# Channel mixer in 1024-column groups, two of eight k-pairs with seven block products

## The chip, the cores and the metric

One core of one Trainium2 chip runs the whole kernel. The metric is the device time of one execution in microseconds (us). Three runs of the kernel before gave 2060.73, 2060.61 and 2063.79 us; their median is 2060.73.

## The reference, cut to what matters

Two decoder layers work on 256 tokens of width 2048 (layer A: sliding-window attention, layer B: block attention over a shared K/V; both with memory heads), each followed by a dense squared-ReLU channel mixer with 8192 hidden columns. The change lies in the mixer and in the normalisation:

```python
h = layer_norm(ALPHA * h + mix, ln_g[layer, 0], ln_b[layer, 0])
ffn = jnp.square(jax.nn.relu(h @ w_up[layer])) @ w_down[layer]
h = layer_norm(ALPHA * h + ffn, ln_g[layer, 1], ln_b[layer, 1])
```

All data are f32.

## The kernel before, in words

**Precision by splitting.** Every operand of a product is kept as a sum of two fp32r tiles: `hi`, a cast made by ScalarE (ACT), and `lo = src - hi`, made by VectorE (DVE); `split` is lines 93 to 95. A product of two blocks takes three matmuls, x_hi w_hi, x_hi w_lo and x_lo w_hi (lines 169 to 171).

**Weights.** `weights` (line 97) fetches 1 MB with one DMA on SyncE's queue (SP) into a `raw` buffer of 128x2048, of which there are four (NRAW), and splits it as two halves of 1024 columns into `whi` and `wlo` buffers, of which there are seven each (NHI). A `raw` buffer is free when its splits are done, a `whi` or `wlo` buffer when its last matmul is done.

**Mixer.** The hidden width is cut into four chunks of 2048 columns (loop at line 482). In a chunk, four up passes (`aform`, line 158) multiply the transposed activations hT (16 k-tiles of 128) with 512 columns each, for both token tiles t = 0 and 1 in two PSUM banks of the pool `ps_mm` (four banks). One weight DMA covers four k-tiles of 512 columns: 24 matmuls. `relu2` (line 383) takes a bank through a ReLU on ACT and a square on DVE into a `u_n` buffer; four PE transposes per tile, placed by the hooks two and five k-tiles into the next pass, bring it into gT through a bank of the pool `ps_at` (four banks), with a cast on ACT and a subtraction on DVE (`transposed`, lines 323 to 330). Four down passes then multiply gT with the matching rows of w_down, and `residual` (line 332) adds each bank into h on DVE. A chunk has 768 matmuls of 512 columns and 32 transposes.

**Normalisation.** `ln_stat` (line 300) computes the inverse root of the variance with three Newton steps on 128x1 tiles: seven GpSimd (POOL) instructions, lines 310 to 314, between two DVE stages. There are four normalisations with two token tiles each. During two of them memory projections (a filler) keep TensorE (PE) at work; in layer 1's first one, and in the last, some of the matmuls of token tile 1 are held back (`hold`) for the same purpose.

**Order.** The tile framework plans each engine's queue at compile time, from the program's order as priority and from what is ready and which buffers are free in its own model; on the chip each queue of ACT, DVE and SP is worked off in that fixed order.

Of the kernel before, what the change touches and what calls it, by code (L numbers as in the profile page):

```python
# [8 lines left out]
F32 = mybir.dt.float32  # L9
# [23 lines left out]
FAR = -1e33  # L33
NRAW = 4
NHI = 7
NLG = 3
HOLD = 13
HOLDF = 14

# [25 lines left out]
WHOOKS = (10, 14, 4)  # L65
NWARM = 2
FILL = (10, 11, 12, 16)
UHOOKS = (2, 5)
WTAIL = ((1, 2), (2, 0), (3, 1), (5, 2), (7, 1), (9, 2))


# [1 line left out]
def trunk(ctx: ExitStack, tc: tile.TileContext, a: dict, out: bass.AP):  # L73
# [19 lines left out]
    def split(hi, lo, src):  # L93
        nc.scalar.copy(hi, src)  # L94
        nc.vector.tensor_tensor(lo, src, hi.bitcast(F32), ALU.subtract)  # L95

    def weights(src, parts=1):

# [59 lines left out]
    def aform(srcs, xts, hold=0, hooks={}):  # L158

        ps = [ps_mm.tile([P, 512], F32, name="ps_a", tag="mm") for _ in range(NT)]
        n = len(srcs)

        def mms(t, k, hi, lo):
            xh = xts[k // 4][:, k % 4, 0, t * P:(t + 1) * P]
            xl = xts[k // 4][:, k % 4, 1, t * P:(t + 1) * P]
            st, en = k == 0, k == 4 * n - 1
            nc.tensor.matmul(ps[t], xh, hi, start=st, stop=False)  # L169
            nc.tensor.matmul(ps[t], xh, lo, start=False, stop=False)  # L170
            nc.tensor.matmul(ps[t], xl, hi, start=False, stop=en)  # L171

        late = []
        for i, src in enumerate(srcs):
            halves = weights(src)
            for q in range(4):
                hi, lo = halves[q // 2]
                c = slice((q % 2) * 512, (q % 2) * 512 + 512)
                args = (4 * i + q, hi[:, c], lo[:, c])
                hooks.get(4 * i + q, nothing)()  # L180
                mms(0, *args)
                if 4 * i + q >= 4 * n - hold:
                    late.append(args)
                else:
                    mms(1, *args)

        def finish():
            for args in late:
                mms(1, *args)

        return ps, finish


    def evict_v(ps, nm):
# [105 lines left out]
    def ln_stat(stats):  # L300

        mv = sm.tile([P, 2], F32, name="mvar", tag="mvar")
        nc.vector.bn_aggr(mv, stats)
        v = sm.tile([P, 1], F32, name="v", tag="v")
        nc.vector.tensor_scalar(v, mv[:, 1:2], EPS, None, op0=ALU.add)
        y = sm.tile([P, 1], F32, name="y", tag="y")
        nc.vector.tensor_scalar(y.bitcast(I32), v.bitcast(I32), -0.5, 1597463007.0,
                                op0=ALU.mult, op1=ALU.add)
        w = sm.tile([P, 1], F32, name="w", tag="w")
        nc.gpsimd.tensor_scalar(w, v, -0.5, None, op0=ALU.mult)  # L310
        u = sm.tile([P, 1], F32, name="u", tag="u")
        for _ in range(3):
            nc.gpsimd.tensor_scalar(u, y, y, w, op0=ALU.mult, op1=ALU.mult)  # L313
            nc.gpsimd.tensor_scalar(y, u, 1.5, y, op0=ALU.add, op1=ALU.mult)
        return mv[:, 0:1], y

    def ln_apply(ht, mean, rstd, rows, j):
# [20 lines left out]
    def new_stats():  # L338
        return [sm.tile([P, 4, 6], F32, name=f"st{t}", tag=f"st{t}", bufs=2) for t in range(NT)]
# [4 lines left out]
    def normed(h, st, li, ps, finish, first, filler):  # L344


        if filler:
            rows = ln_rows(li, [[(wp, "raw", NRAW, D)]] * 2)
        else:
            rows = ln_rows(li, [[(ap_, "mk", 1, 1024), (ap_, "mv", 1, 1024)],  # L350
                                [(ap_, "v", 1, 1024)] + [(ap_, "pts", 2, 512)] * 2])
        xt = []
        if filler:
            finish()
            for t in range(NT):
                residual(h, ps, t, 3, first, st)
                mean, rstd = ln_stat(st[t])
                for j in range(4):
                    ln_apply(h[t], mean, rstd, rows, j)
            done = 0  # L360
            for j, at in enumerate(FILL):
                for _ in range(done, at):
                    next(filler)
                done = at
                xt.append(act_tile("hT", "hT", j))
                for t in range(NT):
                    transposed(h[t][:, j * 512:(j + 1) * 512], xt[j], t, j)
            for _ in filler:
                pass
            return xt  # L370
        for j in range(4):
            xt.append(act_tile("hT", "hT", j))
        for t in range(NT):
            if t:
                finish()
            residual(h, ps, t, 3, first, st)
            mean, rstd = ln_stat(st[t])
            for j in range(4):
                ln_apply(h[t], mean, rstd, rows, j)
                transposed(h[t][:, j * 512:(j + 1) * 512], xt[j], t, j)  # L380
        return xt

    def relu2(ps):

        u = ap_.tile([P, 512], F32, name="u_n", tag="lg", bufs=NLG)
        nc.scalar.activation(u, ps, AF.Relu)
        nc.vector.tensor_tensor(u, u, u, ALU.mult)
        return u
# [59 lines left out]
    for l in range(LAYERS):  # L448
        more = l + 1 < LAYERS
        wq, wk, wv, wqm = (a[f"{n}{l}"] for n in ("wq", "wk", "wv", "wqm"))  # L450
        ps, _ = aform([wv[0, i] for i in range(4)], hT, hooks={6: lambda: next(mem["mk_rest"])})
        v = evict_v(ps, "v")
        ot = new_acts("og", "ot")
        pipe = Stages()
        kt = None
        for g in range(KVH):
            kt = ap_.tile([P, T], F32, name="kt", tag="kt", bufs=2)
            wform_sum(wk[g], hT, kt, pipe.hooks(*WHOOKS))
            for hd in range(g * GROUP, (g + 1) * GROUP):
                qt = new_q()  # L460
                wform_sum(wq[hd], hT, qt, pipe.hooks(*WHOOKS))
                pipe.add(self_head(ot, hd, qt, kt, v, dist_a if l == 0 else dist_b, l == 0))
        if l == 0:
            for t in range(NT):
                h.append(ap_.tile([P, D], F32, name=f"h{t}", tag=f"h{t}"))
                nc.sync.dma_start(h[t], a["x"][t * P:(t + 1) * P, :])
        for m in range(MH):
            qt = new_q()
            wform_sum(wqm[m], hT, qt, pipe.hooks(*WHOOKS))
            pipe.add(mem_head(ot, m, qt, mem["mk"][:, m], mem["mv"]))  # L470
        if more:
            memt = load_acts(a["memt"], "hT", "memt")
        st = new_stats()
        for nb in range(4):
            ps, fin = aform([a["wo"][l, nb, i] for i in range(4)], ot, hold=(0 if nb < 3 else 8 if more else HOLD),
                            hooks=pipe.tail() if nb == 0 else {})
            if nb < 3:
                for t in range(NT):
                    residual(h, ps, t, nb, True, st)
        hT = normed(h, st, 2 * l, ps, fin, True, mem_v(l + 1, memt, mem) if more else None)  # L480
        st = new_stats()
        for c in range(FF // CH):
            gt = new_acts("og", "gT")
            todo = {}
            for nb in range(CH // 512):
                split_t = c == 0 and nb == 0 and not more
                ps, fin = aform([a["wup"][l, c * (CH // 512) + nb, i] for i in range(4)], hT,
                                hold=(16 if split_t else 0), hooks=todo)
                if split_t:
                    u0 = relu2(ps[0])  # L490
                    fin()
                    us = [u0, relu2(ps[1])]
                else:
                    us = [relu2(ps[t]) for t in range(NT)]
                todo = {UHOOKS[t]: (lambda u=us[t], g=gt[nb], t=t: transposed(u, g, t, 0)) for t in range(NT)}
            last = c == FF // CH - 1
            if last and more:
                memt = load_acts(a["memt"], "hT", "memt")
            for nb in range(4):
                end = last and nb == 3  # L500
                ps, fin = aform([a["wdn"][l, nb, 4 * c + i] for i in range(4)], gt,
                                hold=(0 if not end else 8 if more else HOLDF),
                                hooks=(todo if nb == 0 else {}))
                if not end:
                    for t in range(NT):
                        residual(h, ps, t, nb, c == 0, st if last else None)
        if more:
            hT = normed(h, st, 2 * l + 1, ps, fin, False, mem_k(l + 1, memt, mem))
    rows = ln_rows(2 * LAYERS - 1, [[(ap_, f"hT{i}", 1, D)] for i in range(2)])
# [52 lines left out]
```

## Time and profile before

| | us |
|---|---|
| median of three runs | 2060.73 |
| the profiled execution | 2060.95 |
| its span, first to last instruction | 2059.2 |
| granted clock of PE (mean) | 0.996 |

The span is 1.75 us shorter than the time of the same execution. Busy times overlap between engines; a PE record is longer than the distance to the next one, because matmuls are pipelined, so PE's pace is read from start times.

### The profile page before, as it was taken

To read this page: it belongs to the slowest core of one execution; us is meant where nothing else is said; L and a number is where in the kernel's file an instruction comes from. 1 tells how busy PE (TensorE), PEld (TensorE's weight loads), DVE (VectorE), ACT (ScalarE), POOL (GpSimd) and SP (SyncE) were. 2 spreads that over 40 slices of the span, in tenths; PEclk is the share of its full clock that TensorE was granted. 3 is DMA by queue.
4 is the path that set the end of the run, shared out by engine and by line. 5 is a ranking of instruction groups with operands and counts; after the bars stand their busy time and mean duration, and the time that the engine had idled before them with its cause. 6 is when DMAs were issued, how large, how long until landed. Compare 5 with 4: busy or idle time off the path is not lost.

```text
span 2059.2 us, 23603 instructions
## 1 busy us (share of the span) xinstructions
PE 2035.7 (99%) x9500; PEld 1695.2 (82%) x9500; DVE 1176.3 (57%) x1373; ACT 913.2 (44%) x1136; POOL 28.4 (1%) x64
## 2 busy tenths in 40 slices
PE   9999999999999999999999999899999999999997
PEld 7888888888888888888888888788888888888886
DVE  6566657555555555456575665665555555555555
ACT  6555435443443444345344554344344434434441
POOL 0000000000000000000010000100000000000001
PEclk9999999999999999999999999999999999999998
DMA  9644546555555555556554446355555555555651
GB/s 337 255 147 157 200 152 256 181 196 186 186 186 200 184 185 193 194 184 225 199 208 176 154 156 212 123 204 184 194 194 184 185 199 188 185 186 195 230 186 62
DMA packets 56269, 391.60 MB, mean 190 GB/s; under 512 B 6368, under 2 KB 6368, under 8 KB 9696
## 3 DMA queue, kind: packets, MB, share of 16 engines
q1 hardware_dynamic: 56160, 390.10, 53.4%
q8 instruction: 74, 1.21, 0.2%
q14 instruction: 35, 0.29, 0.0%
HBM read 387.98 MB, written 2.10 MB: 189 GB/s over the span
## 4 chain that ended last, share of the span: by engine, by line
PE 95%; DVE 3%; POOL 1%; issue 0%; DMA 0%; SPq 0%; ACT 0%; POOLq 0%; DVEq 0%
PE ps_a L169 26%; PE ps_a L171 26%; PE ps_a L170 26%; PE ps_w L147 7%; PE ps_w L149 4%; PE pt_h L327 2%; PE ps_m L405 1%; PE ps_m L404 1%; PE ps_m L406 1%; DVE h L321 1%; POOL u L313 1%; PE po L234 1%; PE pt L229 1%; PE ps_s L245 1%; DVE wlo L95 0%; DVE h L320 0%
## 5 line engine op out<-in xcount | busy, mean ns | idle before, releaser
L95 DVE TENSOR_TENSOR wlo<-raw,whi 128x1024 fp32r<-128x1024 f32 (+1 forms) x706 | 859.6, 1221 | 776.7 <-ACT whi L94 774.1
L94 ACT CAST whi<-raw 128x1024 fp32r<-128x1024 f32 (+1 forms) x706 | 739.9, 1051 | 946.8 <-PE ps_a L171 828.2
L169 PE MATMUL ps_a<-whi,hT 128*128 128x512 f32 x1056 | 417.3, 395 | 0.0
L170 PE MATMUL ps_a<-wlo,hT 128*128 128x512 f32 x1056 | 412.1, 390 | 0.1
L171 PE MATMUL ps_a<-whi,hT 128*128 128x512 f32 x1056 | 411.9, 390 | 0.0
L169 PE MATMUL ps_a<-whi,gT 128*128 128x512 f32 x1024 | 400.1, 391 | 0.0
L171 PE MATMUL ps_a<-whi,gT 128*128 128x512 f32 x1024 | 398.6, 389 | 0.0
L170 PE MATMUL ps_a<-wlo,gT 128*128 128x512 f32 x1024 | 398.5, 389 | 0.0
L171 PEld LDWEIGHTS ps_a<-whi,hT 128*128 128x128 f32 x1056 | 198.7, 188 | 42.5
L170 PEld LDWEIGHTS ps_a<-wlo,hT 128*128 128x128 f32 x1056 | 198.9, 188 | 40.4 <-DVE wlo L95 0.5
L169 PEld LDWEIGHTS ps_a<-whi,hT 128*128 128x128 f32 x1056 | 198.7, 188 | 40.1 <-ACT hT L329 0.2
L171 PEld LDWEIGHTS ps_a<-whi,gT 128*128 128x128 f32 x1024 | 192.2, 188 | 40.4
L170 PEld LDWEIGHTS ps_a<-wlo,gT 128*128 128x128 f32 x1024 | 192.3, 188 | 39.4
L169 PEld LDWEIGHTS ps_a<-whi,gT 128*128 128x128 f32 x1024 | 192.2, 188 | 39.4
L147 PE MATMUL ps_w<-hT,whi 128*128 128x512 f32 x320 | 119.9, 414 | 0.0
L147 PE MATMUL ps_w<-xT,whi 128*128 128x512 f32 x320 | 119.9, 414 | 0.0
L169 PE MATMUL ps_a<-whi,ot 128*128 128x512 f32 x256 | 101.8, 398 | 0.0
L171 PE MATMUL ps_a<-whi,ot 128*128 128x512 f32 x256 | 99.8, 390 | 0.0
L170 PE MATMUL ps_a<-wlo,ot 128*128 128x512 f32 x256 | 99.8, 390 | 0.0
L149 PE MATMUL ps_w<-xT,wlo 128*128 128x256 f32 x320 | 89.9, 281 | 0.0
L149 PE MATMUL ps_w<-hT,wlo 128*128 128x256 f32 x320 | 89.9, 281 | 0.0
L147 PEld LDWEIGHTS ps_w<-hT,whi 128*128 128x128 f32 x320 | 60.2, 188 | 13.2
(103 smaller groups left out, 1423.1 us busy)
## 6 DMA issues: line engine op xcount, KB each, us to landing
raw<-in_wup_dram SPq DMA_DIRECT2D x128, 1024.0 KB, 4.8
raw<-in_wdn_dram SPq DMA_DIRECT2D x128, 1024.0 KB, 4.8
raw<-in_wo_dram SPq DMA_DIRECT2D x32, 1024.0 KB, 4.8
raw<-in_wq_dram SPq DMA_DIRECT2D x24, 1024.0 KB, 4.8
raw<-in_wmk_dram SPq DMA_DIRECT2D x8, 1024.0 KB, 7.3
raw<-in_wv_dram SPq DMA_DIRECT2D x8, 1024.0 KB, 7.8
raw<-in_wk_dram SPq DMA_DIRECT2D x8, 1024.0 KB, 4.8
raw<-in_wqm_dram SPq DMA_DIRECT2D x8, 1024.0 KB, 4.8
```

The costliest lines, as they stand in the source:

```text
L94: nc.scalar.copy(hi, src)
L95: nc.vector.tensor_tensor(lo, src, hi.bitcast(F32), ALU.subtract)
L147: nc.tensor.matmul(ps, hi[:, kk:kk + P], x.rearrange("p s t -> p (s t)"), start=(k == 0), stop=False)
L149: nc.tensor.matmul(ps[:, :T], lo[:, kk:kk + P], x[:, 0], start=False, stop=(k == KT - 1))
L169: nc.tensor.matmul(ps[t], xh, hi, start=st, stop=False)
L170: nc.tensor.matmul(ps[t], xh, lo, start=False, stop=False)
L171: nc.tensor.matmul(ps[t], xl, hi, start=False, stop=en)
L229: nc.tensor.transpose(pt[:, dst:dst + P], lg[:, c0:c0 + P], ident)
L234: nc.tensor.matmul(po[:, :T], v[:, 0, vcol:vcol + P], pts[:, :T], start=True, stop=False)
L245: nc.tensor.matmul(ps[:, P:3 * P], qt[:, P:], kt, start=True, stop=True)
L313: nc.gpsimd.tensor_scalar(u, y, y, w, op0=ALU.mult, op1=ALU.mult)
L327: nc.tensor.transpose(pt[:, k], src[:, k * P:(k + 1) * P], ident)
```

## The change

The mixer runs in groups of 1024 columns (`mlp_group`), each with four `ps_mm` banks b: token tile b // 2, column half b % 2. A group walks over eight pairs of k-tiles in the order 2, 3, 0, 4, 1, 5, 6, 7. One DMA of 1 MB brings the four 128x512 blocks of a pair, stored as B11, B22, B12, B21 (a new layout made on the host). Six pairs take the eight block products, 24 matmuls. Pairs 0 and 1 take seven, 21 matmuls: `fast_weights` makes seven split blocks from three given and four combined ones, with a second `raw` buffer t for the combinations; `fast_acts` makes the four combinations of activations, once per set of activations, in another `raw` buffer (`x_f`). Three products go to their own banks directly and four to the `ps_at` banks P1, P5, P6 and P7; after the second of these pairs, `early` combines those four on DVE. An up group then adds its four banks, and takes ReLU and square on ACT; a down group adds into h eight times in place of four.

Of 32 groups, three stay as two `aform` passes: the first up group of layer 1 and the last down group of each layer. The seven small instructions of `ln_stat` move from POOL to DVE, a fourth `u_n` buffer is added, and a DMA scratch area is made smaller. The loops of lines 484 to 506 are replaced by the last part of the diff.

```diff
-NLG = 3
+NLG = 4
...
-UHOOKS = (2, 5)
+ORDER = (2, 3, 0, 4, 1, 5, 6, 7)
+FAST = (0, 1)
+UHOOKS = ((0, 3), (1, 0), (1, 2), (1, 3))
...
+    def fast_weights(src):
+        raw = wp.tile([P, 2048], F32, name="raw", tag="raw", bufs=NRAW)
+        nc.sync.dma_start(raw, src)
+        b = raw.rearrange("p (q c) -> p q c", q=4)
+        t_ = wp.tile([P, 4, 512], F32, name="t", tag="raw", bufs=NRAW)
+        tiles = []
+        def pair(s, n):
+            hi = wp.tile([P, 1024], F32R, name="whi", tag="whi", bufs=NHI)
+            lo = wp.tile([P, 1024], F32R, name="wlo", tag="wlo", bufs=NHI)
+            split(hi[:, :n], lo[:, :n], s)
+            tiles.extend([(hi[:, c:c + 512], lo[:, c:c + 512]) for c in range(0, n, 512)])
+        pair(raw[:, :1024], 1024)
+        nc.vector.tensor_tensor(t_[:, 0:2], b[:, 0:2], b[:, 2:3].broadcast_to([P, 2, 512]), ALU.subtract)
+        pair(b[:, 3], 512)
+        pair(t_[:, 0:2].rearrange("p q c -> p (q c)"), 1024)
+        nc.vector.tensor_tensor(t_[:, 2], b[:, 1], t_[:, 0], ALU.add)
+        nc.vector.tensor_tensor(t_[:, 3], b[:, 3], t_[:, 2], ALU.subtract)
+        pair(t_[:, 2:4].rearrange("p q c -> p (q c)"), 1024)
+        return dict(zip(("B11", "B22", "B21", "T1", "T3", "T2", "T4"), tiles))
+    def fast_acts(x, s_):
+        raw = wp.tile([P, 2048], F32, name="x_f", tag="raw", bufs=NRAW)
+        f = raw[:, :1024].rearrange("p (k t) -> p k t", k=4)
+        nc.vector.tensor_tensor(f, x[:, :, 0].bitcast(F32), x[:, :, 1].bitcast(F32), ALU.add)
+        a11, a21 = f[:, 0:4:2, :P], f[:, 0:4:2, P:]
+        a12, a22 = f[:, 1:4:2, :P], f[:, 1:4:2, P:]
+        s = raw[:, 1024:].rearrange("p (q u t) -> p q u t", q=4, u=2)
+        nc.vector.scalar_tensor_tensor(s[:, 0], a21, -1.0, a22, op0=ALU.mult, op1=ALU.subtract)
+        nc.vector.scalar_tensor_tensor(s[:, 1], s[:, 0], -1.0, a11, op0=ALU.mult, op1=ALU.subtract)
+        nc.vector.tensor_tensor(s[:, 2], a11, a21, ALU.subtract)
+        nc.vector.tensor_tensor(s[:, 3], a12, s[:, 1], ALU.subtract)
+        split(s_[:, 0], s_[:, 1], raw[:, 1024:])
...
+    def mlp_group(src, xts, sums, hooks, early):
+        ps = [ps_mm.tile([P, 512], F32, name="ps_g", tag="mm") for _ in range(4)]
+        own = {}
+        seen = {}
+        last = {}
+        fast = ("P1", 0, 1, "P5", "P7", "P6", 2)
+        for u in ORDER:
+            for i in range(7 if u in FAST else 4):
+                last[fast[i] if u in FAST else i] = (u, i)
+        def mm3(bank, x, w, st, en):
+            (xh, xl), (hi, lo) = x, w
+            nc.tensor.matmul(bank, xh, hi, start=st, stop=False)
+            nc.tensor.matmul(bank, xh, lo, start=False, stop=False)
+            nc.tensor.matmul(bank, xl, hi, start=False, stop=en)
+        def tok(k, t):
+            return [xts[k // 4][:, k % 4, s, t * P:(t + 1) * P] for s in range(2)]
+        left = len([u for u in ORDER if u in FAST])
+        for pos, u in enumerate(ORDER):
+            k0, k1 = 2 * u, 2 * u + 1
+            if u in FAST:
+                for i in range(4):
+                    hooks.get((pos, i), nothing)()
+                if not own:
+                    for nm in ("P1", "P5", "P6", "P7"):
+                        own[nm] = ps_at.tile([P, 512], F32, name=nm, tag="at")
+                w = fast_weights(src[u])
+                sx = [[sums[:, s, q, u % 2] for s in range(2)] for q in range(4)]
+                prods = (("P1", tok(k0, 0), "B11"), (0, tok(k1, 0), "B21"), (1, sx[3], "B22"),
+                         ("P5", sx[0], "T1"), ("P7", sx[2], "T3"), ("P6", sx[1], "T2"), (2, tok(k1, 1), "T4"))
+                for i, (b, x, wn) in enumerate(prods):
+                    mm3(own[b] if b in own else ps[b], x, w[wn], b not in seen, last[b] == (u, i))
+                    seen[b] = True
+                left -= 1
+                if not left:
+                    early(own)
+                continue
+            (h0, l0), (h1, l1) = weights(src[u])
+            w = {"B11": (h0[:, :512], l0[:, :512]), "B22": (h0[:, 512:], l0[:, 512:]),
+                 "B12": (h1[:, :512], l1[:, :512]), "B21": (h1[:, 512:], l1[:, 512:])}
+            for b in range(4):
+                hooks.get((pos, b), nothing)()
+                t, n = b // 2, b % 2 + 1
+                mm3(ps[b], tok(k0, t), w[f"B1{n}"], b not in seen, False)
+                mm3(ps[b], tok(k1, t), w[f"B2{n}"], False, last[b] == (u, b))
+                seen[b] = True
+        return ps
...
-        nc.gpsimd.tensor_scalar(w, v, -0.5, None, op0=ALU.mult)
+        nc.vector.tensor_scalar(w, v, -0.5, None, op0=ALU.mult)
         u = sm.tile([P, 1], F32, name="u", tag="u")
         for _ in range(3):
-            nc.gpsimd.tensor_scalar(u, y, y, w, op0=ALU.mult, op1=ALU.mult)
-            nc.gpsimd.tensor_scalar(y, u, 1.5, y, op0=ALU.add, op1=ALU.mult)
+            nc.vector.tensor_scalar(u, y, y, w, op0=ALU.mult, op1=ALU.mult)
+            nc.vector.tensor_scalar(y, u, 1.5, y, op0=ALU.add, op1=ALU.mult)
         return mv[:, 0:1], y
...
+    def sums_up(res):
+        def early(own):
+            u = [ap_.tile([P, 512], F32, name="u_n", tag="lg", bufs=NLG) for _ in range(4)]
+            nc.scalar.copy(u[0], own["P1"])
+            nc.vector.tensor_tensor(u[2], u[0], own["P6"], ALU.add)
+            nc.vector.tensor_tensor(u[1], u[2], own["P5"], ALU.add)
+            nc.vector.tensor_tensor(u[2], u[2], own["P7"], ALU.add)
+            nc.vector.tensor_tensor(u[3], u[2], own["P5"], ALU.add)
+            res.extend(u)
+        return early
+    def sums_down(h, v, first):
+        def early(own):
+            c0 = v * 1024
+            a_ = ALPHA if first else 1.0
+            s1, s2, s4 = (ap_.tile([P, 512], F32, name="u_n", tag="lg", bufs=NLG) for _ in range(3))
+            nc.scalar.copy(s1, own["P1"])
+            c = h[0][:, c0:c0 + 512]
+            nc.vector.scalar_tensor_tensor(c, c, a_, own["P1"], op0=ALU.mult, op1=ALU.add)
+            nc.vector.tensor_tensor(s2, s1, own["P6"], ALU.add)
+            nc.vector.tensor_tensor(s4, s2, own["P5"], ALU.add)
...
+        return early
...
+        sum_h = None
         for c in range(FF // CH):
             gt = new_acts("og", "gT")
+            todo = []
+            sum_g = ap_.tile([P, 2, 4, 2, P], F32R, name="sum_g", tag="sum_g")
+            for v_ in range(CH // 1024):
+                hooks = dict(zip(UHOOKS, todo))
+                us = [None] * 4
+                if c == 0 and v_ == 0 and not more:
+                    for nb in range(2):
...
                 else:
+                    if sum_h is None:
+                        sum_h = ap_.tile([P, 2, 4, 2, P], F32R, name="sum_h", tag="sum_h")
+                        fast_acts(hT[0], sum_h)
+                    acc = []
+                    ps = mlp_group(a["wup"][l, c * (CH // 1024) + v_], hT, sum_h, hooks, sums_up(acc))
+                    for b in range(4):
+                        nc.vector.tensor_tensor(acc[b], acc[b], ps[b], ALU.add)
+                        nc.scalar.activation(acc[b], acc[b], AF.Relu)
+                        nc.scalar.activation(acc[b], acc[b], AF.Square)
+                    us = acc
+                def back(b, v_=v_, us=us, gt=gt, sum_g=sum_g):
+                    transposed(us[b], gt[2 * v_ + b % 2], b // 2, 0)
+                    if v_ == 0 and b == 2:
+                        fast_acts(gt[0], sum_g)
+                todo = [lambda b=b, f=back: f(b) for b in (0, 1, 2, 3)]
...
+            for v_ in range(D // 1024):
+                if last and v_ == 1:
+                    for nb in range(2, 4):
+                        ps, fin = aform([a["wdn_s"][l, nb - 2, i] for i in range(4)], gt,
+                                        hold=(0 if nb == 2 else 8 if more else HOLDF))
+                        if nb == 2:
+                            for t in range(NT):
+                                residual(h, ps, t, nb, False, st)
+                    continue
+                ps = mlp_group(a["wdn"][l, v_, 8 * c:8 * c + 8], gt, sum_g, dict(zip(UHOOKS, todo)),
+                               sums_down(h, v_, c == 0))
+                todo = []
+                for b in range(4):
+                    residual(h, {b // 2: ps[b]}, b // 2, 2 * v_ + b % 2, False, st if last else None)
```

## Rows read from the trace of the kernel before

**Rows 1.** The page, part 1 and part 2 (clock row), whole span.

```profile
PE 2035.7 (99%) x9500; PEld 1695.2 (82%) x9500; DVE 1176.3 (57%) x1373; ACT 913.2 (44%) x1136; POOL 28.4 (1%) x64
...
PEclk9999999999999999999999999999999999999998
```

**Rows 2.** The chain that ended last, by engine (page, part 4).

```profile
PE 95%; DVE 3%; POOL 1%; issue 0%; DMA 0%; SPq 0%; ACT 0%; POOLq 0%; DVEq 0%
```

**Rows 3.** Windows (us; PE, PEld, DVE, ACT busy): one chunk of the channel mixer, layer 0.

```profile
355.07:533.12 178.05, 178.05 (x803) 147.30 (x801) 93.86 (x89) 76.07 (x80) 0.00 (x0) 1.00 0.54 189
```

**Rows 4.** Timeline of ACT inside a down pass (start us, us, engine, line).

```profile
511.39 1.05 ACT L94 CAST whi<-raw 128x1024 fp32r<-128x1024 f32 x1 [1.66 <-PE ps_a L171]
...
516.84 1.05 ACT L94 CAST whi<-raw 128x1024 fp32r<-128x1024 f32 x1 [1.67 <-PE ps_a L171]
```

**Rows 5.** Groups of instructions by line and shape (count, busy us, mean ns, idle before).

```profile
L95 DVE TENSOR_TENSOR wlo<-raw,whi 128x1024 fp32r<-128x1024 f32 x702 | 856.9, 1224 | 774.9 <-ACT whi L94 772.2
L94 ACT CAST whi<-raw 128x1024 fp32r<-128x1024 f32 x702 | 737.4, 1053 | 944.7 <-PE ps_a L171 828.2 <-PE ps_w L147 62.9 <-DMA raw<-in_wmv_dram 15.7
...
L387 DVE TENSOR_TENSOR u_n<-u_n 128x512 f32<-128x512 f32 x64 | 44.0, 692 | 12.7 <-ACT u_n L386 12.7
L386 ACT ACTIVATE u_n<-ps_a 128x512 f32<-128x512 f32 x64 | 38.3, 598 | 37.3 <-PE ps_a L171 34.7
...
L329 ACT CAST gT<-pt_h 128x512 fp32r<-128x512 f32 x64 | 37.3, 583 | 23.1 <-PE pt_h L327 23.1
...
L156 DVE TENSOR_TENSOR qt<-ps_w,sb 128x256 f32<-128x256 f32 x32 | 13.2, 412 | 0.0
...
L94 ACT CAST whi<-raw 128x512 fp32r<-128x512 f32 x4 | 2.5, 619 | 2.1 <-DMA raw<-in_wmv_dram 2.1
...
L94 ACT ACT_TABLE_LOAD x1 | 1.3, 1283 | 0.7 <-PEq L554 0.7
```

**Rows 6.** Timeline of DVE in layer 1's first normalisation.

```profile
1322.67 0.75 DVE L321 SCALAR_TENSOR_TENSOR h<-h,y,ln_row 128x512 f32<-128x512 f32 x1
1323.33 2.36 DVE L95 TENSOR_TENSOR wlo<-raw,whi 128x1024 fp32r<-128x1024 f32 x2
```

**Rows 7.** The DMA queue's own waits, and the DMA issues of the page.

```profile
SPq L103 <- DVE wlo L95: 1698.1, 332, 21.1
...
raw<-in_wup_dram SPq DMA_DIRECT2D x128, 1024.0 KB, 4.8
```

**Rows 8.** Timeline of DVE in the last normalisation, second half.

```profile
2046.34 0.68 DVE L334 SCALAR_TENSOR_TENSOR h<-h,ps_a 128x512 f32<-128x512 f32 x1
...
2047.78 0.26 DVE L303 BATCH_NORM_AGGREGATE mvar<-st 128x2 f32<-128x24 f32 x1
2048.08 0.15 DVE L305 TENSOR_SCALAR v<-mvar 128x1 f32<-128x1 f32 x1
...
2048.81 0.15 DVE L307 TENSOR_SCALAR y<-v 128x1 int32<-128x1 int32 x1
...
2052.42 2.08 DVE L321 SCALAR_TENSOR_TENSOR h<-h,y,ln_row 128x512 f32<-128x512 f32 x3 [2.15 <-POOL y L314]
2054.41 0.75 DVE L320 SCALAR_TENSOR_TENSOR h<-h,mvar,ln_row 128x512 f32<-128x512 f32 x1
```

**Rows 9.** Timeline of POOL in the same stretch, first and last of seven.

```profile
2048.32 0.64 POOL L310 TENSOR_SCALAR w<-v 128x1 f32<-128x1 f32 x1 [5.46 <-DVE v L305]
...
2052.12 0.27 POOL L314 TENSOR_SCALAR y<-u,y 128x1 f32<-128x1 f32 x1
```

**Rows 10.** Timeline of PE in layer 1's first normalisation.

```profile
1319.02 0.66 PE L327 MATMUL pt_h<-ident,h 128*128 128x128 f32 x4 [2.18 <-DVE h L321]
...
1336.13 1.94 PE L327 MATMUL pt_h<-ident,h 128*128 128x128 f32 x8 [3.32 <-DVE h L321]
...
1341.05 0.63 PE L171 MATMUL ps_a<-whi,hT 128*128 128x512 f32 x1
1341.48 0.63 PE L169 MATMUL ps_a<-whi,hT 128*128 128x512 f32 x1
```

More of the change, by code (lines that the diff above doesn't have):

```diff
@@ L191, in aform @@
         return ps, finish
+    def mlp_group(src, xts, sums, hooks, early):
[3 more added lines that the diff above has]
+        last = {}
+        plan = []
+        for u in ORDER:
+            plan.extend([(u, b) for b in range(4)] if u not in FAST else [(u, i) for i in range(7)])
+        fast = ("P1", 0, 1, "P5", "P7", "P6", 2)
+        for u in ORDER:
+            for i in range(7 if u in FAST else 4):
[37 more added lines that the diff above has]
+        return ps
@@ L381, in normed @@
         return xt
+    def sums_up(res):
[18 more added lines that the diff above has]
+            nc.vector.tensor_tensor(s4, s2, own["P5"], ALU.add)
+            c = h[0][:, c0 + 512:c0 + 1024]
+            nc.vector.scalar_tensor_tensor(c, c, a_, s4, op0=ALU.mult, op1=ALU.add)
+            nc.vector.tensor_tensor(s2, s2, own["P7"], ALU.add)
+            c = h[1][:, c0:c0 + 512]
+            nc.vector.scalar_tensor_tensor(c, c, a_, s2, op0=ALU.mult, op1=ALU.add)
+            nc.vector.tensor_tensor(s2, s2, own["P5"], ALU.add)
+            c = h[1][:, c0 + 512:c0 + 1024]
+            nc.vector.scalar_tensor_tensor(c, c, a_, s2, op0=ALU.mult, op1=ALU.add)
+        return early
     def relu2(ps):
@@ L481, in trunk @@
         st = new_stats()
+        sum_h = None
         for c in range(FF // CH):
             gt = new_acts("og", "gT")
[L484 to L492, printed above, removed]
-                else:
-                    us = [relu2(ps[t]) for t in range(NT)]
-                todo = {UHOOKS[t]: (lambda u=us[t], g=gt[nb], t=t: transposed(u, g, t, 0)) for t in range(NT)}
+            todo = []
[5 more added lines that the diff above has]
+                    for nb in range(2):
+                        ps, fin = aform([a["wup_s"][nb, i] for i in range(4)], hT, hold=(16 if nb == 0 else 0))
+                        if nb == 0:
+                            us[0] = relu2(ps[0])
+                            fin()
+                            us[2] = relu2(ps[1])
+                        else:
+                            us[1], us[3] = relu2(ps[0]), relu2(ps[1])
+                else:
+                    if sum_h is None:
[13 more added lines that the diff above has]
+                todo = [lambda b=b, f=back: f(b) for b in (0, 1, 2, 3)]
@@ L498, in trunk @@
                 memt = load_acts(a["memt"], "hT", "memt")
[L499 to L506, printed above, removed]
+            for v_ in range(D // 1024):
[12 more added lines that the diff above has]
+                    residual(h, {b // 2: ps[b]}, b // 2, 2 * v_ + b % 2, False, st if last else None)
         if more:
@@ L533, in rows, with quads @@
             w.reshape(k // 512, 4, P, n // 512, 512).transpose(3, 0, 2, 1, 4)).reshape(n // 512, k // 512, P, -1)
+    def quads(w):
+        k, n = w.shape
+        b = w.reshape(k // 256, 2, P, n // 1024, 2, 512).transpose(3, 0, 2, 1, 4, 5)
+        return np.ascontiguousarray(np.stack([b[:, :, :, 0, 0], b[:, :, :, 1, 1], b[:, :, :, 0, 1], b[:, :, :, 1, 0]],
+                                             axis=3)).reshape(n // 1024, k // 256, P, 2048)
     def act_t(x):
@@ L549 @@
         "wo": np.stack([rows(w) for w in i["w_o"]]),
-        "wup": np.stack([rows(w) for w in i["w_up"]]),
-        "wdn": np.stack([rows(w) for w in i["w_down"]]),
+        "wup": np.stack([quads(w) for w in i["w_up"]]),
+        "wdn": np.stack([quads(w) for w in i["w_down"]]),
+        "wup_s": rows(i["w_up"][-1][:, :1024]),
+        "wdn_s": np.stack([rows(w[FF - CH:, 1024:]) for w in i["w_down"]]),
         "ln_g": np.ascontiguousarray(i["ln_g"]), "ln_b": np.ascontiguousarray(i["ln_b"]),
     }
-    nc = bacc.Bacc("TRN2", target_bir_lowering=False, num_devices=1)
+    nc = bacc.Bacc("TRN2", target_bir_lowering=False, num_devices=1, dynamic_dma_scratch_size=1024)
     args = {k: nc.dram_tensor(f"in_{k}_dram", v.shape, mybir.dt.from_np(v.dtype), kind="ExternalInput").ap()
```

## The prediction

> **What bounds the kernel now.** The page comes first: TensorE is busy for 99% of the span at full granted clock, DVE for 57%, ACT for 44% [rows 1]. The chain that ended last says the same in another way: 95% of it is PE, 3% DVE and 1% POOL [rows 2]. So the mixer is matmul-bound, and what is left over lies in the normalisations. In the mixer, the casts of weights show PE's pace: each waits until a matmul releases a buffer, and they start 2.725 us apart (516.84 - 511.39 = 5.45 for two) [rows 4]. Such a half unit holds 12 matmuls, so one costs 2.725 / 12 = 0.227 us. A whole chunk agrees: it lasts 178.05 us [rows 3]; 768 x 0.227 = 174.3, and the 3.7 left are 32 transposes of 0.12. In that chunk DVE is busy for 93.9 us and ACT for 76.1: 53% and 43%.
>
> A difference of 0.2%, about 4 us, is what a measurement of this kernel can tell from none.
>
> **The matmuls removed.** 29 of the 32 groups become `mlp_group`: 8 up and 7 down in layer 0, 7 and 7 in layer 1. Each has two pairs with seven products instead of eight and so saves 2 x 3 = 6 matmuls: 174 in all, 174 x 0.227 = **39.5 us**. Shapes, columns and weight loads of the others stay the same, so I take the pace as unchanged. The Trainium skill ("TensorE: Matmul & The Clock Gate", Back-to-back issue gap) gives 216 ns for a lone stream of 512-column matmuls and about 131 ns in a stream with weight loads; by these the saving would be 37.6 or 22.8 us. The trace's 227 ns agrees with neither, and decides.
>
> **The vector work added.** Here is the question: does DVE still keep ahead of PE? A 1024-column split costs DVE 1.224 us and ACT 1.053 by itself; 512 columns cost 0.69 and 0.62 [rows 5]. Back to back two DVE splits take 2.36, so they start 1.14 apart [rows 6]. I use the longer figures. An ordinary pair costs DVE 2 x 1.224 = 2.45. A seven-product pair has three and a half splits, 3 x 1.224 + 0.69 = 4.36, and four combined blocks, 1.224 + 2 x 0.69 = 2.60: 6.97. Eight pairs make 6 x 2.45 + 2 x 6.97 = 28.6. An up group adds four sums after the second fast pair, four at the end and four transposed tiles, 12 x 0.69 = 8.3, and half a `fast_acts`: 1.224 for the sum of hi and lo, four blocks of 256 at 0.41 at most, 1.224 for the split, so 4.1 per chunk, 2.0 per up group. In all 39 us. A down group has eight sums, four residuals and on average two transposed tiles, 9.7: 38 us. PE needs 186 x 0.227 = 42.2 us per group, and about 2 more where there are 16 transposes. So DVE is busy for 88 to 91% by the long figures, and about 82% by the back-to-back ones. ACT has 6 x 2.11 + 2 x 3.78 = 20.2 of casts, 0.6 for P1, eight ReLUs and squares of 0.6, four copies of 0.58 and half a cast of 1.05: 28 us, 65%. The trace has a single table load, of 1.283 us, and squares were not on ACT [rows 5]; if each of an up group's eight changes between ReLU and square needed one, ACT would come to 39 us, so between nothing and that it is hidden by PE's 44, and I take nothing. Both engines fit, DVE with little to spare.
>
> Room to run ahead: `whi` buffers are taken in sevens. A fast pair takes four, an ordinary one two, so the seven cover between two fast pairs' half and three and a half ordinary pairs, 9 to 19 us of matmuls; the new order of the products keeps both halves of an ordinary pair to its end, which leaves at worst one unit, 24 x 0.227 = 5.4 us, between the release of a buffer and the first use of its next content (the pairs right after the fast ones). A split needs 1.05 + 1.22 = 2.3 of that. The gap between the two fast pairs (pair 4 lies there) gives DVE 5.4 us to catch up, and the transfer of 4.8 us per MB [rows 7] lies two pairs ahead. The rate of DMA stays at 1 MB per 5 us.
>
> **New waits.** Four `ps_mm` banks now hold one group, with none to spare, so a group's first matmul in bank b waits for the eviction of that bank. Bank 0 is complete 18 matmuls, 4.1 us, before the group's end, and the others follow every 1.36 us; an eviction on DVE takes 0.69. Cost nothing, hidden by those 18 matmuls; without the cover it would be about 1 us per group. The `ps_at` banks of P1 to P7 wait for the transposed tiles just ahead: the last transposition is 6 matmuls before the first fast product, and P7, the last bank, is first needed 12 matmuls later: 18 x 0.227 = 4.1 us against a cast and a subtraction, 0.58 + 0.69. Nothing again. ReLU and square become two ACT instructions; the square tile is needed 18 matmuls after the group's end, against 0.69 + 2 x 0.6 of work. Nothing.
>
> What remains are the places where a queue runs into the wrong order, the first group after a normalisation (its buffers are empty, and DVE has 4.1 us more for `fast_acts`), and the two changes from `aform` to groups. No row shows them. The bounds are nothing, and 1.5 us in each of 29 groups, about one `whi` split with its cast missed every time, 43 us; I take **2 us**, near nothing, because ACT's casts now wait 828 us in sum for PE, not the other way [rows 5], and SP waits 1698 us for splits [rows 7].
>
> **The normalisation.** From the end of `y` at 2048.96 to the first use at 2052.42 pass 3.46 us, in which DVE sits idle for 2.15 [rows 8], and POOL runs from 2048.32 to 2052.39 [rows 9]. On DVE seven such instructions take 0.15 each and start 0.03 after the one they depend on (2047.78 + 0.26, then 2048.08) [rows 8]: 7 x 0.18 = 1.3 us in series, 0.5 if laid between the other DVE work. The gain is 0.9 to 1.6 per token tile. It counts where DVE's end is the end: in the last tile (the first one there ends at 2046.34, as the held matmuls do [rows 8]), and twice in layer 1's first normalisation, where PE is idle for 2.18 and 3.32 us [rows 10]. Three times 0.9 to 1.6, and nothing to 2 for the two with a filler: 2.7 to 6.8. I take **3 us**, the serial end. After the longer idle time PE runs at the lower of its two clock levels, 1.2 GHz: matmuls start 0.43 apart [rows 10], not 0.227. If a shorter idle time spares that, some 2 us more are won; only the range has them. No queue is passed by this move: POOL has nothing else there.
>
> **Sum.** -39.5 - 3 + 2 = -40.5 us. The profiled execution would go from 2060.95 to 2020.45 (span 2059.2 to 2018.7). That execution is 0.2 above the median, so I say 2020.2.
>
> **Rivals.**
> 1. *Slower: the `raw` buffers are handed out in the program's order* (0.13). `x_f` of the next down groups is named between pairs 3 and 0 of the chunk's second up group, but first written only when gT's first block stands: 36 matmuls, 12 transposes, a cast and a subtraction after the group's start, 8.2 + 1.5 + 1.3 = 11 us. If the transfers named after it can't go ahead, pair 0's lands at 15.8. Then a cast, a split, the combination and the next cast (1.05 + 1.22 + 1.22 + 1.05) lead to 20.3, where PE wanted P5's weights at 57 matmuls and 16 transposes, 14.9: 5.4 us lost. Pair 1's transfer, two behind it, loses about 3 more. Eight such groups cost 64 to 80 us and give 2085 to 2100. It decides from 5.3 us per such group on. For it: one pool, four buffers, one SP queue. Against it: queues are planned by what is ready, as splits of later weights between DVE's normalisation steps show [rows 6].
> 2. *Partly given back: DVE falls behind in the fast pairs* (0.15). DVE works in a fixed order: a fourth line 320 ran only at 2054.41, behind three of line 321 that waited for POOL, though it needs nothing from POOL [rows 8]. Within a fast pair, with nothing else laid between, DVE waits for ACT's cast of the first combinations, 1.05 less the 0.69 of the single block's split, and for the whole cast of the second, 1.05: 1.4 us, 2.8 per group. On top of 38 to 39 us that makes 41 to 42 of PE's 42.2 to 44.2, and what comes unevenly is lost: 0.5 to 1 us per group, 15 to 29 in all, give 2034 to 2048. The Trainium skill ("PSUM — Partial Sum Buffer", Engine vs sequencer instructions) calls the queues of ScalarE, VectorE and GpSimd strict FIFO; by that rule alone this rival would be the likelier one. The trace agrees with the order, but DVE's overlap of back-to-back splits (1.14 for 1.224) and the seven buffers speak for the forecast.
> 3. *Hardly a change* (0.03): the same loss at 1.3 to 1.5 us per group eats nearly everything, 2057 to 2064.
>
> That the change doesn't do what it says would show in PE's instruction count: 174 fewer matmuls are certain from the loops.
>
> **Numbers.** Forecast, 2012 to 2030: 0.68. With rival 2's 0.15 faster comes to 0.83; same is rival 3's 0.03, slower rival 1's 0.13 and 0.01 for both mishaps of DVE at once. The range runs from 2012 (saving 39.5, normalisation 6.8, clock 2) to rival 2's end at 2048; it leaves out rivals 1 and 3.
>
> **What would show it.** Right: an up group without the first of a layer lasts 44.2 us and a down group with transposes the same, without them 42.2; ACT's casts still wait for PE; DVE is busy near 80% in the mixer; POOL has no Newton steps. Wrong: PE idle before a matmul on a P5 or P6 bank, put down to DVE's `wlo` or ACT's `whi`; SP waiting on `x_f`; DVE back to back through whole groups. A pace other than 0.227 would change the first term.

## The result and the profile after

The changed kernel takes **2084.06 us** (2082.79 to 2085.73, four runs) against 2060.74 of the kernel before: 1.011 of its time, 95% interval 1.0093 to 1.0128. It is 23 us slower, where the forecast was 2020.2, faster, with a range up to 2048. One later execution (2573.74 us at a granted clock of 0.729, of the kernel that names the sum later) is left out of every ratio.

The page of the changed kernel (span, busy times, chain), the lines that answer to [rows 1, 2]:

```profile
span 2083.6 us, 23980 instructions
...
PE 2023.7 (97%) x9326; PEld 1675.4 (80%) x9326; DVE 1540.2 (74%) x1951; ACT 1045.6 (50%) x1351; POOL 1.2 (0%) x8
...
PE 92%; DVE 6%; ACT 1%; issue 0%; DMA 0%; SPq 0%; DVEq 0%; ACTq 0%
```

PE executes the 174 matmuls less (9326 in place of 9500), but its share falls from 99% to 97% while DVE's rises from 57% to 74%, and in the chain 1% is now ACT. The window of one chunk, from one stall to the next (us; PE, PEld, DVE, ACT, POOL busy; clock, DMA), answers to [rows 3]; the second window is a piece near its start:

```profile
391.24:572.05 180.81, 176.02 (x777) 144.44 (x777) 141.89 (x159) 93.91 (x110) 0.00 (x0) 0.98 0.52 186
394.36:399.25 4.89, 4.89 (x13) 3.83 (x12) 3.75 (x6) 2.38 (x3) 0.00 (x0) 0.50 0.26 107
```

The chunk lasts 180.81 us; before it was 178.05, and with 24 matmuls fewer it should be 178.05 - 24 x 0.227 = 172.6. So 8.2 us are lost, and the clock is no longer full: 0.98 on average, 0.50 in the second window. PE's waits in the whole span (us in total, times, longest) say where:

```profile
PE P L254 <- ACT whi L96: 38.3, 16, 3.5
```

Sixteen waits of PE, two in each of eight chunks, all for the cast of a weight block of a seven-product pair, in the chunk's second up group. The timeline of PE around the first of them (start, us, engine, line; idle time and releaser in brackets), and then the chain there (start, us to the next step):

```profile
391.24 0.50 PE L254 MATMUL P<-whi,hT 128*128 128x512 f32 x1 [3.51 <-ACT whi L96]
...
393.76 0.80 PE L254 MATMUL P<-whi,sum_h 128*128 128x512 f32 x1 [1.27 <-ACT whi L96]
```

```profile
393.76 0.80 PE P L254
...
398.82 0.43 PE P L256
399.25 0.37 PE P L254
399.63 0.47 PE ps_g L254 x2
400.09 0.23 PE P L255
```

PE is idle for 3.51 and 1.27 us, 4.78 together. Afterwards matmuls start 0.43 us apart, the lower of the two clock levels (1.2 GHz), until 399.25, and 0.23 after that. From 393.76 to 399.63 thirteen matmuls start in 5.87 us, where 13 x 0.227 = 2.95 would do: 2.9 of the remaining 8.2 - 4.8 = 3.4 us are this half clock. The last 0.5 lies in the three matmuls between the two waits, which take 1.25 us in place of 0.68.

Why is the cast late? The same stretch on ACT, DVE and the DMA queue:

```profile
376.38 0.63 ACT L641 ACTIVATE u_n<-u_n 128x512 f32<-128x512 f32 x1
...
384.53 0.59 ACT L428 CAST gT<-pt_h 128x512 fp32r<-128x512 f32 x1 [2.60 <-PE pt_h L426]
...
389.19 1.04 ACT L96 CAST sum_g<-x_f 128x1024 fp32r<-128x1024 f32 x1 [2.24 <-DVE x_f L136]
390.14 1.56 ACT L96 CAST whi<-raw 128x1024 fp32r<-128x1024 f32 x2
```

```profile
385.14 0.69 DVE L429 TENSOR_TENSOR gT<-pt_h,gT 128x512 fp32r<-128x512 f32 x1 [2.50 <-ACT gT L428]
385.87 1.22 DVE L129 TENSOR_TENSOR x_f<-gT 128x1024 f32<-128x1024 f32 x1
...
390.27 1.23 DVE L97 TENSOR_TENSOR sum_g<-x_f,sum_g 128x1024 fp32r<-128x1024 f32 x1 [1.11 <-ACT sum_g L96]
```

```profile
363.31 0.33 SPq L104 DMA_DIRECT2D raw<-in_wup_dram  x1
...
391.52 0.33 SPq L104 DMA_DIRECT2D raw<-in_wup_dram  x1
```

Pair 0's transfer (line 104, `fast_weights`) was issued at 363.31; at the 4.9 us of the page it had landed before 369. Yet its first cast stands at 390.14 on ACT, right behind the cast of `sum_g` at 389.19, which waits for `x_f`, which waits for the third transposed tile of gT at 385.14. Between 377.0 and 384.5 ACT had no work but the casts of two other tiles. So the data were there, ACT was free, and the queue's fixed order kept pair 0 behind `x_f`. The Trainium skill ("PSUM — Partial Sum Buffer", Engine vs sequencer instructions) calls ACT's and DVE's queues strict FIFO; these rows agree.

### The profile page after: what moved, and what is told of

Same layout as the page of the kernel before. It is cut to its first block, busy times and chain, and to the rows that moved or that the text cites. A ratio compares the mean times of both kernels' runs of the same rounds, so it can differ in the third digit from the quotient of the medians.

```text
span 2083.6 us, 23980 instructions
## 1 busy us (share of the span) xinstructions
PE 2023.7 (97%) x9326; PEld 1675.4 (80%) x9326; DVE 1540.2 (74%) x1951; ACT 1045.6 (50%) x1351; POOL 1.2 (0%) x8
## 4 chain that ended last, share of the span: by engine, by line
PE 92%; DVE 6%; ACT 1%; issue 0%; DMA 0%; SPq 0%; DVEq 0%; ACTq 0%
PE ps_g L256 17%; PE ps_g L255 17%; PE ps_g L254 17%; PE ps_w L189 7%; PE ps_a L211 5%; PE ps_a L212 5%; PE ps_a L213 5%; PE ps_w L191 4%; PE P L254 3%; PE P L256 3%; PE P L255 3%; PE pt_h L426 2%; PE ps_m L536 1%; PE ps_m L538 1%; PE ps_m L537 1%; DVE h L419 1%
## 5 line engine op out<-in xcount | busy, mean ns | idle before, releaser
L255 PE MATMUL ps_g<-wlo,hT 128*128 128x512 f32 x780 | 305.8, 392 | 0.1
L256 PE MATMUL ps_g<-whi,hT 128*128 128x512 f32 x780 | 305.9, 392 | 0.0
L254 PE MATMUL ps_g<-whi,hT 128*128 128x512 f32 x780 | 302.6, 395 | 0.9 <-ACT whi L96 0.7
L254 PE MATMUL ps_g<-whi,gT 128*128 128x512 f32 x728 | 285.3, 393 | 0.0
L256 PE MATMUL ps_g<-whi,gT 128*128 128x512 f32 x728 | 283.5, 390 | 0.0
L255 PE MATMUL ps_g<-wlo,gT 128*128 128x512 f32 x728 | 283.4, 390 | 0.0
L96 ACT CAST whi<-t 128x1024 fp32r<-128x1024 f32 x116 | 122.0, 1052 | 120.9 <-PE ps_g L256 45.0
L254 PEld LDWEIGHTS ps_g<-whi,hT 128*128 128x128 f32 x780 | 147.8, 190 | 33.7 <-ACT whi L96 3.8
L255 PEld LDWEIGHTS ps_g<-wlo,hT 128*128 128x128 f32 x780 | 147.7, 189 | 31.3 <-DVE wlo L97 0.5
L256 PEld LDWEIGHTS ps_g<-whi,hT 128*128 128x128 f32 x780 | 147.6, 189 | 31.0
L97 DVE TENSOR_TENSOR wlo<-t,whi 128x1024 fp32r<-128x1024 f32 x116 | 141.6, 1223 | 41.2 <-ACT whi L96 40.9
L256 PEld LDWEIGHTS ps_g<-whi,gT 128*128 128x128 f32 x728 | 136.7, 188 | 28.8
L255 PEld LDWEIGHTS ps_g<-wlo,gT 128*128 128x128 f32 x728 | 136.8, 188 | 27.6
L254 PEld LDWEIGHTS ps_g<-whi,gT 128*128 128x128 f32 x728 | 136.6, 188 | 27.2
```

Source lines behind the costliest of these rows:

```text
L254: nc.tensor.matmul(bank, xh, hi, start=st, stop=False)
L255: nc.tensor.matmul(bank, xh, lo, start=False, stop=False)
L256: nc.tensor.matmul(bank, xl, hi, start=False, stop=en)
```

## The experiments

**The sum of activations in buffers of its own.** `fast_acts` uses two buffers that are idle in the mixer:

```diff
-        raw = wp.tile([P, 2048], F32, name="x_f", tag="raw", bufs=NRAW)
-        f = raw[:, :1024].rearrange("p (k t) -> p k t", k=4)
+        f = ap_.tile([P, 4, T], F32, name="x_f", tag="mk")
...
-        s = raw[:, 1024:].rearrange("p (q u t) -> p q u t", q=4, u=2)
+        x_s = ap_.tile([P, 1024], F32, name="x_s", tag="v")
+        s = x_s.rearrange("p (q u t) -> p q u t", q=4, u=2)
```

> x_f and its four combinations get buffers of their own (those of mk and v, idle during the mixer) instead of one of the four raw buffers; place in the program and DVE work stay the same. Theory A (queue order): because x_f is named in the raw ring before pair 0's transfer, the planner puts the casts and splits of pair 0 behind x_f on ACT and DVE, and PE waits 3.5 + 1.3 us and then runs at the lower clock; a chunk lasts 180.8 us instead of 768 - 24 = 744 matmuls x 0.227 + 3.9 = 172.6. Without the shared ring each of eight chunks gives 8.2 us back: 2084 - 66 = 2018 us. Theory B (DVE load): DVE is late because of the 4.1 us that fast_acts and the 14 us that fast pairs add; they are unchanged here, so 2075 to 2085 us.

Measured: **2015.12 us** (2014.57 to 2016.68), 0.9778 of before (0.9765 to 0.9791). Its chunk (from the first matmul behind a seven-product pair to the same one a chunk later), all of PE's waits in the span, and ACT's timeline at the same place in the program:

```profile
398.79:571.29 172.50, 172.50 (x777) 142.81 (x776) 142.07 (x159) 93.55 (x110) 0.00 (x0) 1.00 0.53 195
```

```profile
PE pt_h L426 <- DVE h L420: 3.7, 2, 2.0
PE ps_m L536 <- ACT whi L96: 2.2, 1, 2.2
PE ps_warm L93 <- DVE warm L90: 1.5, 1, 1.5
```

```profile
373.95 1.04 ACT L96 CAST whi<-t 128x1024 fp32r<-128x1024 f32 x1
...
377.15 1.05 ACT L96 CAST whi<-t 128x1024 fp32r<-128x1024 f32 x1
...
387.71 1.05 ACT L96 CAST sum_g<-x_s 128x1024 fp32r<-128x1024 f32 x1
```

The chunk lasts 172.50 us with PE at full clock throughout, 0.1 less than the sum above. None of the sixteen waits is left. Pair 0's casts (two `whi<-t` at 373.95 and 377.15) are done before `sum_g` is even started, although DVE's busy time per chunk is the same, 142.1 us against 141.9. Theory B falls.

**The same buffer, named later.** `fast_acts(gt[0], sum_g)` moves from `back` to the head of pair 5:

```diff
                 hooks = dict(zip(UHOOKS, todo))
+                if v_ == 1:
+                    hooks[(5, 0)] = lambda gt=gt, sum_g=sum_g: fast_acts(gt[0], sum_g)
```

> fast_acts for the down groups keeps its raw buffer but is named three pairs later, at the head of pair 5 of the second up group, behind both fast pairs. Theory A (queue order): nothing of the fast pairs is named behind x_f, gT's first block has long been standing, so the stall goes: 2018 us. Its sum is due only at pair 0 of the down group, 28 us later, so nothing new waits. Theory B (DVE load): the same work in the same group, 2070 to 2085 us.

Measured: 2015.98 us (0.9782, 0.9769 to 0.9795). The stall is gone with `x_f` still in the raw ring, that is, in one of the four `raw` buffers.

**The fast pairs later in the group.**

```diff
-ORDER = (2, 3, 0, 4, 1, 5, 6, 7)
+ORDER = (2, 3, 4, 5, 0, 6, 1, 7)
```

> The changed kernel with the two seven-product pairs at the fifth and seventh place of a group instead of the third and fifth (order 2, 3, 4, 5, 0, 6, 1, 7). x_f is now named just ahead of pair 4, an ordinary pair. Theory A (queue order): PE waits before pair 4 instead of pair 0, as its casts now stand behind x_f: at least 3 us idle in eight chunks and the lower clock after it, 2060 to 2084 us. Theory B (load, or the long chain of a fast pair behind x_f): two ordinary pairs more, 10.9 us, cover it: 2018 to 2030 us.

Measured: 2071.18 us (1.0048, 1.0034 to 1.0062). PE's waits, and the first of them:

```profile
PE ps_g L254 <- ACT whi L96: 28.8, 9, 3.5
PE ps_g L255 <- DVE wlo L97: 4.7, 9, 0.7
```

```profile
388.91 1.22 PE L254 MATMUL ps_g<-whi,hT 128*128 128x512 f32 x2 [3.51 <-ACT whi L96]
```

The same 3.51 us now stand before `ps_g`, an ordinary pair's first matmul. It is not the fast pair's long chain of casts that is late, but whatever is named behind `x_f`. The second wait is not that chain's either: 0.23 to 0.7 us for an ordinary pair's split, instead of 1.27 for a cast of combined blocks.

**A buffer written early.** The last question was how `x_f` holds up the others: because it takes one of four buffers, or because in the plan its buffer is handed out only when its first instruction can run.

```diff
         raw = wp.tile([P, 2048], F32, name="x_f", tag="raw", bufs=NRAW)
+        nc.gpsimd.memset(raw[:, :1], 0.0)
```

> The changed kernel as it was measured (x_f in the raw ring, at its place), with one POOL instruction more: it writes one column of x_f's buffer as soon as the buffer is free, without waiting for any data; the sum then overwrites it. Theory (the planner hands out the raw buffers in the program's order, and x_f's late first write holds up, in the plan, everything named after it): the buffer is handed out at once, pair 0's casts move ahead of x_f, and most of the 66 us come back: 2015 to 2030 us; what may stay is pair 1's transfer, which waits for x_f's release. Rival (a lack of a fourth raw buffer while x_f stands): x_f now holds it even longer, 2084 us or more.

Measured: **2015.09 us** (0.9775, 0.9758 to 0.9791). POOL's early write, and two casts of ACT at the same place in the program:

```profile
354.87 0.10 POOL L128 MEMSET x_f<- 128x1 f32 x1 [42.10 <-DVE wlo L97]
```

```profile
376.15 1.05 ACT L96 CAST whi<-t 128x1024 fp32r<-128x1024 f32 x1
...
386.78 1.05 ACT L96 CAST sum_g<-x_f 128x1024 fp32r<-128x1024 f32 x1
```

One column written by POOL without any data to wait for brings back all of it, with the buffer held longer, and pair 0's casts stand ahead of `sum_g` again. So it is no lack of a buffer; it is the order that the plan makes when `x_f`'s first write comes late, as a hand-out in the program's order would. How the planner comes to it was not traced further.

**The normalisation alone**, the kernel before with lines 310 to 314 on DVE:

> The kernel before, with only the seven small instructions of the normalisation on DVE. The prediction's term: -3 us, 2057.7 us (2.7 to 6.8 less than 2060.7). Read from the traces: last tile 0.9 us, layer 1's first normalisation 1.8 us of idle time and about 2 us of the lower clock: 2056 us. Rival: the engines around them set the end, 2060.7 us.

Measured: 2055.01 us against 2061.21 in the same session (0.9973, 0.9962 to 0.9983): 6.2 us, by the interval 3.5 to 7.8, where the term was 3. PE's waits for DVE in the kernel before, then in this one:

```profile
PE pt_h L327 <- DVE h L321: 5.5, 2, 3.3
PE ps_m L405 <- DVE wlo L95: 2.3, 2, 1.1
```

```profile
PE pt_h L327 <- DVE h L321: 4.5, 3, 2.2
```

The starts of the same matmuls in the two traces say where it is won. This kernel is 1.23 us late ahead of layer 0's first normalisation (290.03 before, 291.26 here), 0.11 ahead after it (341.31, 341.20), 1.34 ahead after the second (1200.04, 1198.70) and 3.46 ahead after layer 1's first (1400.07, 1396.61); its span ends 4.2 earlier. So the four normalisations give 1.3, 1.2, 2.1 and 0.7 us, 5.4 in all. The first two had each held PE up for 1.15 us, for a split of the filler's weights that stood on DVE behind the wait for POOL; those waits are gone. In layer 1's first one PE is idle for 2.04 and 2.20 us in place of 2.18 and 3.32; the lower clock still follows, for a shorter time (mean granted clock from 1300 to 1350 us: 0.97 in place of 0.93). The chain of small steps itself became no shorter. DVE in the last tile:

```profile
2045.34 0.14 DVE L307 TENSOR_SCALAR y<-v 128x1 int32<-128x1 int32 x1
...
2048.30 0.27 DVE L313 TENSOR_SCALAR u<-y,w 128x1 f32<-128x1 f32 x1
2048.61 0.21 DVE L314 TENSOR_SCALAR y<-u,y 128x1 f32<-128x1 f32 x1
2048.86 2.74 DVE L321 SCALAR_TENSOR_TENSOR h<-h,y,ln_row 128x512 f32<-128x512 f32 x4
```

From the end of `y` to the first use pass 3.38 us, against 3.46 before [rows 8]; steps that need each other start 0.25 to 0.31 apart. What is won is DVE's idle time: other work now lies between the steps.

**Groups without fast pairs** (`FAST = ()`, ReLU straight from the bank, no sums):

> The kernel of the own-buffer run with no seven-product pairs: groups of 1024 columns, new weight layout, ReLU and square on ACT, normalisation on DVE, but 24 matmuls in all eight pairs. Theory: the groups cost nothing and the 174 matmuls are the whole gain: 2015.1 + 174 x 0.227 = 2054.6 us, the same as the norm-only run's 2055.0. Rival: the four-bank groups cost or win something by themselves, then it lies away from 2055 by that much.

Measured: 2054.28 us. Against the own-buffer run the 174 matmuls, net of all the combining work, are worth 39.2 us; against the norm-only run's 2055.01 the groups themselves are worth nothing that can be told.

**More work for DVE** in each fast pair, one and three instructions of 1024 columns:

```diff
         nc.vector.tensor_tensor(t_[:, 0:2], b[:, 0:2], b[:, 2:3].broadcast_to([P, 2, 512]), ALU.subtract)
+        nc.vector.tensor_tensor(t_[:, 2:4], b[:, 0:2], b[:, 2:3].broadcast_to([P, 2, 512]), ALU.subtract)
```

> The own-buffer kernel with one more DVE instruction of 1024 columns in each of 58 fast pairs; it writes what a later one overwrites. DVE's busy time in a chunk goes from 142.2 to 142.2 + 8 x 1.14 = 151.3 us of 172.6 (88%). Theory (DVE has room, PE sets the time): 2015 us, no change. Rival (DVE in fixed order is already the limit in the fast pairs): 58 x 1.14 = 66 us more at most, 2030 to 2081 us.

> The same with three more DVE instructions in each fast pair: 142.2 + 24 x 1.14 = 169.6 us per chunk of 172.6 (98%). Theory: the room is used up; uneven stretches now reach PE, 1 to 3 us per group: 2040 to 2100 us. Rival (buffers even everything out): 2015 to 2020 us.

Measured: 2015.3 us with one, no change; 2033.19 with three, just under what was expected. Of the latter, a quarter of a chunk's time behind the up groups, the PE waits that make up most of the idle time new in it, and one of them:

```profile
443.15:486.30 43.15, 43.15 (x192) 35.72 (x191) 41.20 (x45) 19.45 (x21) 0.00 (x0) 1.00 0.52 195
```

```profile
PE P L257 <- ACT whi L96: 7.7, 8, 1.8
```

```profile
578.05 0.50 PE L257 MATMUL P<-whi,sum_h 128*128 128x512 f32 x1 [0.83 <-ACT whi L96]
```

With DVE busy for 41.2 of 43.15 us (95%) PE runs on in that stretch. But in each chunk of layer 0 it waits 0.83 to 0.98 us in the second seven-product pair of the second up group, and a chunk there takes 2.3 us more than in the own-buffer kernel. By the starts of the same matmuls, 16.7 of the 19.1 us between the two kernels' profiled executions are lost in layer 0's mixer, most in its first and its last chunk, and 2.3 in the last chunk of layer 1.

**Three pairs of eight with seven products:**

> The own-buffer kernel with three of eight pairs taking seven products (pairs 0, 1 and 2, order 3, 2, 4, 0, 5, 1, 6, 7), the third pair's combined activations in idle buffers. 29 x 3 = 87 matmuls fewer, 19.7 us: 1995 us if PE still sets the time. DVE needs about 142.2 + 4 x 4.1 + 2.6 = 161 us per chunk of PE's 169.9 (95%), so theory says part of it is given back: 1996 to 2015 us. Rival (DVE sets the time): above 2015 us.

Measured: 2031.91 us (0.9858), 17 us slower than with two pairs: the rival. PE's longest wait, three of ACT's, and one line of the own-buffer kernel to compare:

```profile
PE P L271 <- ACT whi L96: 13.4, 8, 2.0
```

```profile
ACT whi L96 <- DVE t L116: 192.5, 59, 8.0
ACT whi L96 <- DVE t L120: 157.6, 71, 3.5
...
ACT whi L96 <- PE ps_g L273: 62.9, 36, 3.4
```

```profile
ACT whi L96 <- PE ps_g L256: 441.7, 145, 3.7
```

With two pairs ACT's casts wait 442 us for PE to free buffers, which is room to run ahead; with three it is 63, and ACT waits 350 us for DVE's combined blocks instead. PE's waits for these casts and splits come to 17 us, and its mean granted clock is 0.989 in place of 0.996, by estimate 0.007 x 2032 = 14 us more. The 19.7 us of matmuls saved are more than given back. Whether another order of the pairs would keep some of it was not tried.

## Why the prediction was wrong, point by point

- **The matmuls removed**, 39.5 us: measured 39.2, net of the combining work. Right, and the pace of 0.227 held. Of the two figures of the Trainium skill ("TensorE: Matmul & The Clock Gate", Back-to-back issue gap) the 216 ns, 37.6 us, came near; the 131 ns, 22.8 us, is not borne out.
- **The vector work**: 82% of a chunk by the back-to-back starts; measured 142.1 of 172.5, 82.4%. That it hides behind PE is shown by the run with one instruction more. ReLU and square in turn needed no table loads: the changed kernel's trace has one, as before. Rival 2 fell, at this load.
- **The new waits** for banks: nothing, and PE shows none in the own-buffer run. Right.
- **What remains, 2 us**: this step failed. The prediction took "places where a queue runs into the wrong order" as near nothing, with a bound of 1.5 us in each of 29 groups. It was 8.2 us in eight: 4.8 idle, 2.9 at the lower clock and 0.5 between the waits, 66 us; the runs give 2084.06 - 2015.1 = 69. Of the 70.3 us between the profiled executions of the changed and the own-buffer kernel, the starts of the same matmuls put 67 on these eight places, 1.7 on the first 14 us of the span and 1.4 on the first up group of layer 0, before which PE waits 0.7. The reason given, that ACT waited for PE and SP for splits, described queues of the kernel before, in which every raw buffer is first written by a transfer that needs nothing else. `x_f` was the first whose first writer waits for PE.
- **Rival 1** named the cause and, within 1 us, the time, 2085 to 2100, at a chance of 0.13. Its working was right in the point that decides, `x_f` named before pair 0 and first written at about 11 us, and wrong in the way there: pair 0's transfer was not late on the chip, since SP needs only a free buffer; its casts were late, as the plan had put them behind `x_f`. It counted 8 to 10 us of waiting and no clock; there were 4.8, and that the clock made up most of the rest, and so the time came out, is luck. Two of the prediction's own signs of being wrong are there: PE idle for ACT's `whi` before a P bank, and SP waiting on `x_f`. The latter is the wait for its last reader, the split into `sum_g`: eight waits for pair 1's transfer, which did not reach PE:

```profile
SPq L104 <- DVE sum_g L97: 144.3, 8, 21.9
```

- **The argument against rival 1**, that splits of later weights stood between the normalisation's steps [rows 6], was no evidence: those instructions had their buffers. It shows that the plan goes by what is ready among them, not how a ring of buffers is handed out.
- **The normalisation**, 3 us: mis-sized, measured 6.2 (5.4 in the traces), at the upper end of its 2.7 to 6.8, and that it lies inside the range is partly luck. The working had the seven steps shrink to 0.5 to 1.3 us at 0.18 each; steps that need each other start 0.25 to 0.31 apart, and from `y` to its first use still pass 3.38 us. The gain is the work that fills DVE's wait: 2.5 us where there is a filler, taken as nothing to 2, then 2.1 in layer 1's first and 0.7 in the last tile.

The version with `x_f` in its own buffers, or with the one early write, is 45 to 46 us faster than the kernel before: the change as predicted, with 5 us more.

## What to carry to other kernels

Before a tile joins a ring that also feeds transfers, ask who writes it first and what that writer waits for: here the plan put the casts and splits of the block named after it, in ACT's and DVE's queues, behind that wait, though the data had landed in time. When a wait looks impossible because data and engine were both free, compare the queue's order with the landing times. Price an idle time of some microseconds on PE with its clock as well: here 4.8 us of idle time came with 2.9 at the lower clock.

## What was not expected of the hardware

The length of an idle time did not settle what the clock did after it. In layer 1's first normalisation of the changed kernel PE is idle for 2.04 and then for 1.64 us. The timeline and the chain behind them:

```profile
1336.58 1.32 PE L426 MATMUL pt_h<-ident,h 128*128 128x128 f32 x8 [2.04 <-DVE h L420]
...
1351.87 1.29 PE L426 MATMUL pt_h<-ident,h 128*128 128x128 f32 x8 [1.64 <-DVE h L420]
```

```profile
1340.69 0.43 PE ps_a L212
1341.12 0.43 PE ps_a L213
...
1354.80 0.23 PE ps_a L212
1355.03 0.23 PE ps_a L213
```

After 2.04 us matmuls start 0.43 apart, after 1.64 us 0.23. Before the change 2.18 us had left the clock up and 3.32 had not [rows 10] (in that kernel's chain the matmuls after 1321.37 start 0.23 apart). In the normalisation-only kernel the same 2.04 us left it up (matmuls at 1324.20 and 1324.43), and 2.20 us did not (1338.86 and 1339.28). In the mixer 3.51 and 1.27, with three matmuls between, brought it down until about 399.4, some 6 us. What else decides was not tested. And DVE could be busy for 95% of a quarter of a chunk, in fixed order and with casts of ACT between, without PE waiting there; at the second seven-product pair of an up group the same load did make it wait.
